# A hybrid-attention layer on one core: TensorE in program order along a reckoned clock, attention in three tasks

## The chip, the cores and the metric

The kernel runs on one core of one Trainium2 chip. The metric is device time in microseconds (us), the median of three runs; less is better. Beside each run stands one profiled execution with its trace.

## The reference

One layer of a streaming encoder for 1088 tokens: 1024 of a new prompt and 64 of a stream that goes on, with 512 cached tokens. Everything is fp32.

```python
h = x + 0.5 * rmsnorm(swiglu(rmsnorm(x, g_pre_ff1), w_gate1, w_up1, w_down1), g_post_ff1)
m, rows = token_mix(rmsnorm(h, g_pre_mix), ...)
h = h + rmsnorm(m, g_post_mix)
h = h + 0.5 * rmsnorm(swiglu(rmsnorm(h, g_pre_ff2), w_gate2, w_up2, w_down2), g_post_ff2)
return rmsnorm(h, g_final), rows
# swiglu: (silu(x @ w_gate) * (x @ w_up)) @ w_down        1024 -> 2816 -> 1024
# token_mix: 8 heads of latent attention (softmax, masked by chunks of 64 tokens) and 8 heads of
#   stick-breaking attention (strictly causal, weights from a reversed running sum of log sigmoids),
#   an RMS norm for each head, and one output projection
```

## The kernel before

**Numbers.** Every fp32 operand of a large product is split into a high and a low part (`split`, L121 and L122), and a product is three matmuls (`mm3`): high by high, high by low, low by high. `mul` (L132, L133) issues one matmul, `turn_over` (L137) one transpose on TensorE.

**Groups and stages.** The tokens are two groups: G1 with 576 tokens (moving chunks of 288) and G2 with 512 (one chunk). Two streams of work share TensorE: the feed-forward blocks, whose sums lie in the four PSUM buffers of tile `f`, and the mixing block (norms, projections, attention, output projection) in the single buffers of the tiles `v`, `t` and `s`. Below, F is a matmul of the feed-forward stream, and M is one of the mixing stream. By time: first feed-forward of G1 (0 to 447 us); mixing of G1 beside the first feed-forward of G2 (447 to 1161); mixing of G2 beside the second feed-forward of G1 (1161 to 1967); second feed-forward of G2 (1967 to the end).

**What sets the order.** `weave` takes steps of the mixing stream and puts steps of the feed-forward stream between them, by shares of counted work (`SHARE`). This is the order in which the program is written; the Tile scheduler then orders the instructions of every engine, TensorE's too, when the program is built, and each engine runs its list in that order. The feed-forward block stops before its last second-product part until the mixing block beside it is through (`while end and not self.mixed: yield None`).

**Feed-forward (`ffn`).** For two tiles of 128 hidden features at a time: gate and up products, silu, and the second product (`down`), which sums two tiles in PSUM (six matmuls) and is then added to y by VectorE (L265). Weights come as 128x512 loads `wr` (L241) that ScalarE and VectorE split into `wh` and `wl`.

**Mixing of a group.** `project` makes queries, keys and values, and stores keys and values to DRAM (the last ones by `latent_kv`, L451 and L452). `attend` walks over pairs of heads: `load_keys` reads the keys back from DRAM and splits them (L465 to L473), scores go to tile `s` on TensorE, `stick` (L510 to L532) or `soft` make weights `a` out of them on ScalarE and VectorE (three buffers `a`), and `weighted` turns the weights over (tile `t`), splits them into `ph` (ScalarE, L563) and `pl` (VectorE, L564), and multiplies with the values (tile `v`). `headnorm` sums squares in tile `v`. `mix_out` makes the output projection, a norm over its features, and then, for each of eight tiles of features, `residual`: a load of the saved h into `e` (L232), y * r (L233), y + e (L234), a store of the new h (L796), and a sum of squares (L186, L187). The SP queue has the next load `e<-h` behind the store of the tile before:

```python
nc.sync.dma_start(x, res)                                                    # L232
nc.vector.scalar_tensor_tensor(y, y, self.gain(name, k), r, ...)             # L233
eng.tensor_tensor(y, y, x, op=ALU.add)                                       # L234
if gi == 0: nc.sync.dma_start(self.h2[:, k], y[:, k])                        # L796, in mix_out
self.square(tmp, r2, y[:, k], k == 0)
```

`rsqrt` puts the sum of squares through TensorE with a matrix of ones (`v<-acc,ones` after the output projection, `s<-rx,ones` after the residual, `<-tmp,ones` at the start of a mixing block).

Of the kernel before, what the change touches and what calls it, by code (L numbers as in the profile page):

```python
# [7 lines left out]
F32 = mybir.dt.float32  # L8
# [7 lines left out]
P = 128  # L16
# [18 lines left out]
# token groups: (first token, tokens, chunk of the moving axis). The tokens lie as  # L35
# the first half of the prompt, the sample, the second half of the prompt.
# [4 lines left out]
# TensorE work of the feed-forward stream for one unit of the mixing stream's, part by part  # L41
SHARE = (0.1, 1.5, 0.1, 0.1, 1.2, 0.1)
PACE = 1.0
# [6 lines left out]
class Layer:  # L50
    def __init__(self, tc, ctx, a):
# [5 lines left out]
        self.work = self.share = self.debt = 0.0  # L57
        self.pace = PACE
# [26 lines left out]
        # keys and values: group 1 (prompt | new), group 2, cached  # L85
# [28 lines left out]
    # x = hi + lo exactly; without x, lo holds the value and is replaced in place  # L114
# [12 lines left out]
    # TensorE work is counted, for the interleaving of the two streams  # L127
    def mul(self, out, lhsT, rhs, start, stop):
# [3 lines left out]
        self.work += n / 2400 * (4 if rhs.dtype == F32 else 1)  # L132
        self.nc.tensor.matmul(out, lhsT=lhsT, rhs=rhs, start=start, stop=stop)  # L133

    def turn_over(self, out, x, ident):
        self.work += 0.1
        self.nc.tensor.transpose(out, x, ident)  # L137
# [5 lines left out]
    # a step without TensorE work in the first stream makes room for some of the second's  # L143
    def breath(self):
        self.debt += self.pace
        return True

    # the steps of the first stream, with the second one's between them: self.share of its work each
    def weave(self, first, second):
        mark = self.work  # L150
        for _ in first:
            self.debt += (self.work - mark) * self.share
            mark = self.work
            while self.debt > 0 and next(second, None):
                self.debt -= self.work - mark
                mark = self.work
# [7 lines left out]
    # a bank of the feed-forward stream  # L164
# [3 lines left out]
    # a bank of the mixing stream  # L168
# [10 lines left out]
    # sum of squares, tile by tile  # L179
# [9 lines left out]
    # 1 / sqrt(mean over all features + eps), on every partition, from the sums of squares  # L189
# [9 lines left out]
    # the same with the sums over the tiles left to TensorE (T at most 512)  # L199
# [10 lines left out]
    # tmp() gives [P, T] tiles  # L210
    def rms(self, tmp, bank, tiles, T, width, r=None):
# [33 lines left out]
    def ffn(self, pool, tmp, n, g, xhi, xlo, y, end=None, tail=None):  # L245
# [51 lines left out]
        while end and not self.mixed:  # L297
            yield None
# [799 lines left out]
```

## Time and profile before

| | |
|---|---|
| time, median of 3 (range) | 2368.68 us (2367.98 to 2368.76) |
| span of the profiled execution | 2367.6 us |
| TensorE: matmuls / weight loads | 2283.5 us (96%) / 2033.4 us (86%), 13869 of each |
| VectorE | 1539.0 us (65%) |
| ScalarE | 1244.7 us (53%) |
| GpSimd | 93.6 us (4%) |
| HBM | 227.61 MB read, 40.88 MB written, 113 GB/s over the span |

The profiled execution's span and the median of the runs lie 1.1 us apart. Busy times are sums over the span; matmuls overlap their weight loads, and a matmul that waits inside the engine's pipeline still counts as busy. The chain of work that ended last is TensorE for 69%, VectorE for 12%, ScalarE for 9%, and DMA for 4% of the span.

### The profile page before, as it was taken

The numbers are of one execution on the slowest core, as the hardware profiler recorded it, in microseconds if no ns is written. First come the engines' busy times: TensorE is split into PE (matmuls) and PEld (weight loads), VectorE is DVE, ScalarE is ACT, GpSimd is POOL, SyncE is SP. The second block draws the span as 40 slices with busy tenths as digits, with TensorE's granted clock in tenths as the row PEclk, the third lists the DMA queues.
The fourth block names the chain that finished last, engine by engine and source line by source line (L and its number), as shares of the span: only waits on it lengthen the run. The fifth ranks groups of instructions, "written<-read, shape, count | busy, mean of one in ns | idle before, by whom it ended". The sixth has DMA issues, their size and how long they took to land.

```text
span 2367.6 us, 37687 instructions
## 1 busy us (share of the span) xinstructions
PE 2283.5 (96%) x13869; PEld 2033.4 (86%) x13869; DVE 1539.0 (65%) x2743; ACT 1244.7 (53%) x2459; POOL 93.6 (4%) x270
## 2 busy tenths in 40 slices
PE   8999999989999999999999999999999999999997
PEld 7999999879987777788778999998888888888885
DVE  5555555764277878855873488888878588555555
ACT  6543333453367777754542477777776455433333
POOL 1000000010000000000110000000000010000001
PEclk9999999999999999999999999999999999999998
DMA  6322222445453343343444632323221424333321
GB/s 210 97 95 90 81 80 90 148 144 168 161 150 113 110 129 100 95 151 111 151 142 160 188 96 79 99 72 99 72 86 62 144 81 139 128 98 98 98 90 36
DMA packets 186615, 268.81 MB, mean 114 GB/s; under 512 B 59216, under 2 KB 68048, under 8 KB 186400
## 3 DMA queue, kind: packets, MB, share of 16 engines
q1 hardware_dynamic: 186432, 266.41, 35.8%
q8 instruction: 110, 1.80, 0.3%
q14 instruction: 73, 0.60, 0.1%
HBM read 227.61 MB, written 40.88 MB: 113 GB/s over the span
## 4 chain that ended last, share of the span: by engine, by line
PE 69%; DVE 12%; ACT 9%; DMA 4%; issue 4%; SPq 1%; POOL 1%; DVEq 0%; ACTq 0%; POOLq 0%
PE f L133 46%; PE s L133 11%; PE v L133 6%; PE t L133 3%; PE t L137 2%; DVE a L526 2%; DVE a L529 1%; ACT wh L121 1%; DVE a L520 1%; ACT a L517 1%; DVE wl L122 1%; ACT a L518 1%; ACT a L519 1%; DVE y L265 1%; DVE e L224 1%
## 5 line engine op out<-in xcount | busy, mean ns | idle before, releaser
L133 PE MATMUL f<-xh,wh 128*128 128x288 f32 (+1 forms) x2112 | 695.3, 329 | 4.4 <-ACT xh L121 2.8
L133 PE MATMUL f<-xl,wh 128*128 128x288 f32 (+1 forms) x2112 | 694.3, 329 | 2.9 <-POOL xl L122 1.8
L133 PE MATMUL f<-xh,wl 128*128 128x288 f32 (+1 forms) x2112 | 692.8, 328 | 0.0
L121 ACT CAST wh<-wr 128x512 fp32r<-128x512 f32 x638 | 374.2, 617 | 524.9 <-PE f L133 376.5
L122 DVE TENSOR_TENSOR wl<-wr,wh 128x512 fp32r<-128x512 f32 x638 | 431.2, 698 | 233.0 <-ACT wh L121 208.7
L133 PEld LDWEIGHTS f<-xl,wh 128*128 128x128 f32 x2112 | 397.7, 188 | 33.7 <-POOL xl L122 3.4
L133 PEld LDWEIGHTS f<-xh,wh 128*128 128x128 f32 x2112 | 397.6, 188 | 33.3 <-ACT xh L121 3.3
L133 PEld LDWEIGHTS f<-xh,wl 128*128 128x128 f32 x2112 | 397.5, 188 | 28.1 <-issue 0.8
L133 PE MATMUL f<-hh,wh 128*128 128x288 f32 (+2 forms) x1072 | 350.7, 328 | 6.6 <-ACT hh L121 3.2
L133 PE MATMUL f<-hl,wh 128*128 128x288 f32 (+2 forms) x1072 | 350.7, 327 | 0.0
L133 PE MATMUL f<-hh,wl 128*128 128x288 f32 (+2 forms) x1072 | 349.9, 327 | 0.2 <-DVE wl L122 0.2
L265 DVE TENSOR_TENSOR y<-f,y 128x288 f32<-128x288 f32 (+2 forms) x488 | 247.9, 523 | 85.4 <-PE f L133 83.8
L133 PEld LDWEIGHTS f<-hh,wh 128*128 128x128 f32 x1072 | 201.7, 189 | 23.4 <-ACT hh L121 4.0
L133 PEld LDWEIGHTS f<-hh,wl 128*128 128x128 f32 x1072 | 202.1, 189 | 14.3 <-issue 1.0
L133 PEld LDWEIGHTS f<-hl,wh 128*128 128x128 f32 x1072 | 202.1, 189 | 13.8 <-issue 0.8
L293 DVE TENSOR_TENSOR act<-f,act 128x288 f32<-128x288 f32 (+1 forms) x132 | 70.0, 531 | 92.6 <-PE f L133 91.8
L564 DVE TENSOR_TENSOR pl<-t,ph 128x384 fp32r<-128x384 f32 (+1 forms) x160 | 101.2, 633 | 35.6 <-ACT ph L563 31.2
L563 ACT CAST ph<-t 128x384 fp32r<-128x384 f32 (+1 forms) x160 | 86.7, 542 | 57.2 <-PE t L137 54.7
L292 DVE TENSOR_TENSOR act<-f,act 128x288 f32<-128x288 f32 (+1 forms) x132 | 69.8, 529 | 66.5 <-ACT act L291 66.4
L137 PE MATMUL t<-c_ident,a 128*128 128x128 f32 x616 | 106.0, 277 | 2.7 <-ACT a L531 0.9
L133 PE MATMUL s<-kh,qh 128*128 128x256 f32 (+3 forms) x224 | 84.4, 378 | 24.0 <-DVE a L529 16.1
L121 ACT CAST hh<-act 128x288 fp32r<-128x288 f32 (+1 forms) x132 | 64.8, 491 | 66.0 <-DVE act L293 65.9
(312 smaller groups left out, 3464.7 us busy)
## 6 DMA issues: line engine op xcount, KB each, us to landing
wr<-in_wg SPq DMA_DIRECT2D x176, 256.0 KB, 2.9
wr<-in_wu SPq DMA_DIRECT2D x176, 256.0 KB, 3.0
wr<-in_wd SPq DMA_DIRECT2D x176, 256.0 KB, 3.2
wr<-in_win SPq DMA_DIRECT2D x44, 256.0 KB, 3.3
kl<-ks SPq DMA_DIRECT2D x64, 128.0 KB, 2.8
wr<-in_wout SPq DMA_DIRECT2D x32, 256.0 KB, 2.8
h<-y SPq DMA_DIRECT2D x16, 288.0 KB, 2.3
p<-in_xT SPq DMA_DIRECT2D x16, 256.0 KB, 3.4
```

What stands on the lines that cost most here:

```text
L121: nc.scalar.copy(hi, x)
L122: eng.tensor_tensor(lo, x, f(hi), op=ALU.subtract)
L133: self.nc.tensor.matmul(out, lhsT=lhsT, rhs=rhs, start=start, stop=stop)
L137: self.nc.tensor.transpose(out, x, ident)
L224: self.nc.vector.scalar_tensor_tensor(x, src(k), self.gain(name, k), r, op0=ALU.mult, op1=ALU.mult)
L265: nc.vector.tensor_tensor(yy, ps[:, :C], yy, op=ALU.add)
L292: nc.vector.tensor_tensor(s, pg[:, :C], s, op=ALU.mult)
L293: nc.vector.tensor_tensor(s, pu[:, :C], s, op=ALU.mult)
L517: nc.scalar.activation(av, z, AF.Abs)
L526: nc.vector.tensor_tensor_scan(a[:, j0:n - 1][:, ::-1], zz[:, ::-1], a[:, j0:n - 1][:, ::-1], BIG, op0=ALU.add, op1=ALU.subtract)
L563: nc.scalar.copy(ph[:, end:], tr[:, end:])
L564: nc.vector.tensor_tensor(pl[:, end:], tr[:, end:], f(ph[:, end:]), op=ALU.subtract)
```

## The change

TensorE's order is no longer the scheduler's: the program runs under a manual schedule for that engine, which then executes its instructions as written; the other engines are scheduled as before. `weave`, the shares and the debts go. In their place a clock is kept that adds a price for each matmul. `wait(t)` issues feed-forward steps until the clock reaches t; if the feed-forward stream has no step to give, the clock is set to t. `done(t)` is the same with 4 us of head start (`AHEAD`). Norms, residuals and projections wait at reckoned times. `attend` becomes three tasks, each with a due time: `blocks` (scores and weights, up to six buffers `a`, `RING`), `products` (transposes and the product with the values), and `normed` (the norms of the heads, whose sum of squares now lies in tile `t`). The due task of the lowest number goes next; if none is due, `wait` pulls feed-forward steps. In the feed-forward blocks the second product sums four tiles of hidden features in PSUM (`GROUP`, twelve matmuls) where it summed two, weights are kept in units of 512 columns with eight buffers, and hidden tiles with five.

```diff
-SHARE = (0.1, 1.5, 0.1, 0.1, 1.2, 0.1)
+GROUP = 4
+AHEAD = 4.0
+RING = 6
+SLACK = 1.15
+EARLY = 8
+BLOCKED = object()
...
-    def weave(self, first, second):
-        for _ in first:
-            self.debt += (self.work - mark) * self.share
-            mark = self.work
-            while self.debt > 0 and next(second, None):
-                self.debt -= self.work - mark
-                mark = self.work
+    def wait(self, t):
+        while self.clock < t:
+            mark = self.clock
+            if next(self.filler, BLOCKED) is BLOCKED:
+                self.clock = max(t, mark)
+
+
+    def done(self, t):
+        self.wait(t - AHEAD)
+        return t
...
-        for m in range(0, FT, 2):
+        def product(part, ws, first, dt, c0, C):
+            ps = self.bank_f()
+            ks = slice(dt % H * P, dt % H * P + P)
+            for i, ((wh, wl), (_, hh, hl)) in enumerate(zip(ws, part)):
+                self.mm3(ps[:, :C], wh[:, ks], wl[:, ks], hh[:, c0:c0 + C], hl[:, c0:c0 + C],
+                         i == 0, i == len(part) - 1)
+            yield True
...
+        def down(part, first):
+            for half in range(2):
+                ws = [self.unit(pool, wd[mi][:, half * 512:half * 512 + 512]) for mi, _, _ in part]
+                for dt in range(half * H, half * H + H):
+                    for c0 in range(0, T, C):
+                        yield from product(part, ws, first, dt, c0, C)
...
+        for m in range(0, FT, GROUP):
+            for mi in range(m, min(m + GROUP, FT)):
+                if mi == m + 1 and pend:
+                    yield from down(pend.pop(0), m == GROUP)
...
         while end and not self.mixed:
-            yield None
+            yield BLOCKED
-        yield from down(pend.pop(0), False, order, end)
+        yield from down_last(pend.pop(0), tail, end)
...
+        nc = self.nc
+        a = pool.tile([P, self.keys], F32, name="a", bufs=RING)
...
+    def chain(self, mla, n):
+        act, dve = n / 1200 + 0.35, n / 960 + 0.25
+        if mla:
+            t = 0.6 + dve + act + 0.3
+            return SLACK * t, SLACK * t
+        t = 0.8 + 3 * act + dve + 2 * dve + 0.2
+        return SLACK * t, SLACK * (t + act)
...
         for j in range(0, tiles, 2):
             t = turned(j)
-            yield
+            self.used += 2 if j + 2 == tiles else 0
             if pend:
                 product(*pend)
-                yield
+            yield self.clock + SLACK * 1.9
...
+            e = self.sum_rows(pool, total.rearrange("p b h -> p (b h)"), 4)
+            turned = self.psa.tile([P, 4, P], F32, name="t")
+            for b in range(4):
+                self.turn_over(turned[:, b], e[:, b].rearrange("p h d -> p (h d)"), self.ident)
+            turned = turned.rearrange("p b q -> p (b q)")
...
-        ps = self.psa.tile([P, 512], F32, name="v")
+        yield self.clock + SLACK * (0.3 + n / 500)
+        ps = self.psa.tile([P, 512], F32, name="t")
...
+        first, second, third = ([self.clock, g] for g in (self.blocks(pool, gi), self.products(), self.normed()))
+        while True:
+            tasks = []
+            if first[1] and self.made - self.used < RING:
+                tasks.append((first[0], 0, first))
+            if second[1] and (self.going or self.queue):
+                tasks.append((second[0] if self.going else max(second[0], self.queue[0][0]), 1, second))
+            if third[0] is not None and (self.norming or self.norms):
+                tasks.append((third[0] if self.norming else max(third[0], self.norms[0][0]), 2, third))
+            if not tasks:
+                break
+            due = [t for t in tasks if t[0] <= self.clock]
+            if due:
+                task = min(due, key=lambda t: t[1])[2]
+                task[0] = next(task[1], None)
+                if task[0] is None:
+                    task[0], task[1] = 0.0, None
+            else:
+                self.wait(min(t[0] for t in tasks))
...
+                free, there = self.chain(mla, n)
+                there += self.clock
+                    self.queue.append((there, self.weighted(pool, ab, v, par, b0 + 2 * qp + 2, out, par, then)))
+                self.made += 1
+                yield self.clock + free
...
+        self.wait(self.clock + SLACK * (3 * T / 1000 + 1.0))
         self.rsqrt(bank, s1, T, D, s1)
...
-            yield self.breath()
+            t = self.done(t + SLACK * (2.7 * T / 960 + 0.4))
+        self.wait(t + 2.0)
         self.rsqrt(bank, r2, T, D, r2)
...
-    sizes = {"wr": 4, "wl": 4, "wh": 4, "hh": 3, "hl": 3}
+    sizes = {"wr": 4, "wl": 8, "wh": 8, "hh": GROUP + 1, "hl": GROUP + 1}
...
-    L.weave(mix0(), first)
+
+    first = L.ffn(F, fact, 1, G2, *x1, y1, end=prep2)
+    L.filler = first
+    at = finish(0, y0, 1, L.bank_m)
...
-        with ExitStack() as ctx:
+        with ExitStack() as ctx, tc.manual_schedule(engines={mybir.EngineType.PE}):
```
What the change does to TensorE's list where the first scores of G2's attention are. `wh, lh, ll` are the weights and latent of the last projection (values), `kh, qh` the keys and queries of the first head, `xh, xl` the feed-forward's input. Before:

```order
L133 MATMUL s<-wh,lh 128x512
L133 MATMUL s<-wh,ll 128x512
L133 MATMUL s<-wl,lh 128x512
L133 MATMUL f<-xl,wh 128x288
L133 MATMUL f<-xh,wl 128x288
L133 MATMUL f<-xh,wh 128x288
```

These three F rows are the first of 121 that stand there before the first `s<-kh,qh`. With the change:

```order
L148 MATMUL s<-wh,lh 128x512
L148 MATMUL s<-wh,ll 128x512
L148 MATMUL s<-wl,lh 128x512
L148 MATMUL s<-kh,qh 128x320
L148 MATMUL s<-kh,ql 128x320
L148 MATMUL s<-kl,qh 128x320
```

The 121 F rows between the last projection and the first scores are gone from this place. In G1's attention it is the same with 46 F rows.

TensorE's list after G1's output projection, between the norm over its features (`acc,ones`) and the norm over the new h (`rx,ones`). Before, the first rows of it, and the last:

```order
L133 MATMUL v<-acc,ones 128x288
L133 MATMUL t<-acc,ones 128x288
L133 MATMUL f<-hl,wh 128x512
L133 MATMUL f<-hh,wl 128x512
...
L133 MATMUL f<-hl,wh 128x512
L133 MATMUL s<-rx,ones 128x288
```

With the change, all of it:

```order
L148 MATMUL v<-acc,ones 128x288
L148 MATMUL t<-acc,ones 128x288
L148 MATMUL f<-xh,wh 128x512
L148 MATMUL f<-xl,wh 128x512
L148 MATMUL f<-xh,wl 128x512
L148 MATMUL f<-xh,wh 128x512
L148 MATMUL f<-xl,wh 128x512
L148 MATMUL f<-xh,wl 128x512
L148 MATMUL f<-xh,wh 128x512
L148 MATMUL f<-xl,wh 128x512
L148 MATMUL f<-xh,wl 128x512
L148 MATMUL s<-rx,ones 128x288 x2
```

There were 151 F rows between the two norms, and now there are nine. From there to the next norm (`v<-tmp,ones`) there are now 108, and between the same two norms of G2 (`acc,ones` to `rx,ones`) 159.

SP's queue at the same place, with the loads of the saved h (`h_0`) and the stores of the new one. Before:

```order
L232 DMA e<-h_0_71 128x576 x2
L796 DMA h_73<-y 128x576 x2
L232 DMA e<-h_0_71 128x576
L796 DMA h_73<-y 128x576
L232 DMA e<-h_0_71 128x576
L241 DMA wr<-in_wd 128x512 x2
L796 DMA h_73<-y 128x576
```

With the change:

```order
L254 DMA e<-h_0_73 128x576 x2
L272 DMA wr<-in_wu 128x512
L930 DMA h_75<-y 128x576 x2
L254 DMA e<-h_0_73 128x576
L930 DMA h_75<-y 128x576
L254 DMA e<-h_0_73 128x576
L272 DMA wr<-in_wu 128x512
L930 DMA h_75<-y 128x576
```

A load of h still stands behind the store of the tile before; the weight loads between them are fewer.

TensorE's list in G1's attention, where a head's norm comes due (`osq` squares, `c_blk` the matrix that sums them, `c_ident` the transposes). With the change:

```order
L148 MATMUL v<-aT,v 128x64 x10
L152 MATMUL t<-c_ident,a 128x128 x3
L148 MATMUL t<-osq,c_blk 128x512
L148 MATMUL s<-kh,qh 128x512
L148 MATMUL s<-kh,ql 128x512
```

The norm's sum, which stood in tile `v`, stands in the one buffer of tile `t` right behind transposes into it. 17 of the 24 norms of both attentions stand so.

## Rows read from the trace of the kernel before

**Rows 1.** The page: span, busy time of each engine, and the additions into y.

```profile
span 2367.6 us, 37687 instructions
PE 2283.5 (96%) x13869; PEld 2033.4 (86%) x13869; DVE 1539.0 (65%) x2743; ACT 1244.7 (53%) x2459; POOL 93.6 (4%) x270
...
L265 DVE TENSOR_TENSOR y<-f,y 128x288 f32<-128x288 f32 (+2 forms) x488 | 247.9, 523 | 85.4 <-PE f L133 83.8
```

**Rows 2.** Windows by stage, whole core; the columns are in the first line.

```profile
core 0: us, PE busy (x) PEld busy (x) DVE busy (x) ACT busy (x) POOL busy (x), PEclk, DMA share, GB/s
447.00:650.20 203.20, 194.01 (x1222) 174.30 (x1221) 98.01 (x152) 84.13 (x161) 9.30 (x6) 0.99 0.49 161
650.20:661.00 10.80, 10.63 (x48) 8.47 (x46) 4.79 (x9) 5.41 (x11) 0.70 (x6) 1.00 0.61 173
661.00:1035.00 374.00, 365.53 (x1879) 289.17 (x1880) 297.29 (x603) 269.98 (x614) 17.46 (x118) 1.00 0.40 117
...
1096.10:1136.20 40.10, 36.10 (x156) 28.53 (x154) 31.55 (x49) 18.93 (x33) 4.49 (x2) 1.00 0.58 182
1136.20:1174.20 38.00, 36.35 (x190) 30.67 (x190) 32.73 (x48) 23.72 (x46) 5.98 (x4) 1.00 0.32 101
...
1335.10:1351.10 16.00, 16.00 (x123) 16.00 (x122) 10.07 (x19) 9.39 (x21) 0.00 (x0) 1.00 0.85 239
1351.10:1837.50 486.40, 467.67 (x3329) 437.93 (x3328) 397.51 (x708) 348.05 (x623) 14.39 (x96) 1.00 0.28 85
...
1902.30:1931.90 29.60, 27.50 (x200) 26.53 (x199) 27.73 (x49) 14.97 (x30) 3.41 (x2) 1.00 0.37 116
```

**Rows 3.** Windows of two stretches with feed-forward alone, 288 and 512 wide.

```profile
200.00:400.00 200.00, 200.00 (x1511) 200.00 (x1510) 104.12 (x207) 72.27 (x151) 0.00 (x0) 1.00 0.26 85
2100.00:2200.00 100.00, 100.00 (x443) 82.81 (x442) 50.83 (x79) 33.95 (x61) 0.00 (x0) 1.00 0.30 98
```

**Rows 4.** Timeline from G2's last projection to its first scores (start us, us, engine, line).

```profile
1334.83 0.39 PE L133 MATMUL s<-wl,lh 128*128 128x512 f32 x1
...
1335.31 0.69 DVE L451 COPY e<-s 128x512 f32<-128x512 f32 x1 [0.32 <-PE s L133]
...
1348.69 1.05 ACT L121 CAST kh<-kl 128x1024 fp32r<-128x1024 f32 x1
```

**Rows 5.** Timeline of SP's queue in the residual after G1's output projection.

```profile
1108.07 0.32 SPq L796 DMA_DIRECT2D h<-y  x1
1108.48 0.38 SPq L232 DMA_DIRECT2D e<-h  x1
...
1112.29 0.33 SPq L796 DMA_DIRECT2D h<-y  x1
...
1134.63 0.32 SPq L796 DMA_DIRECT2D h<-y  x1
```

**Rows 6.** Windows of tile f alone: residual of G1, the next norm, the residual of G2.

```profile
1096.10:1136.20 40.10, 35.51 (x151) 28.11 (x151) 8.55 (x14) 1.18 (x2) 1.00 0.58 182
1136.20:1174.20 38.00, 35.72 (x185) 30.09 (x185) 8.64 (x14) 1.41 (x3) 1.00 0.32 101
...
1902.30:1931.90 29.60, 27.00 (x197) 26.18 (x196) 6.80 (x17) 1.22 (x3) 1.00 0.37 116
```

**Rows 7.** Waits of PE in the two attentions: us in total, times, longest.

```profile
PE s L133 <- DVE a L526: 6.5, 18, 0.6
...
PE s L133 <- DVE a L529: 15.8, 25, 2.0
```

**Rows 8.** One line's instructions: duration ns min/median/max, L563 and L564.

```profile
L563 ACT CAST ph<-t x160: 459/579/601, 667.4 to 1832.9; 128x512 fp32r<-128x512 f32 x96, 128x384 fp32r<-128x384 f32 x64
...
L564 DVE TENSOR_TENSOR pl<-t,ph x160: 529/680/693, 667.9 to 1833.4; 128x512 fp32r<-128x512 f32 x96, 128x384 fp32r<-128x384 f32 x64
```

**Rows 9.** Windows around the start of G2's mixing; PEclk is the granted clock.

```profile
1190.00:1197.00 7.00, 4.35 (x33) 4.04 (x31) 5.95 (x9) 2.87 (x6) 1.44 (x1) 1.00 0.79 258
1197.00:1203.80 6.80, 4.95 (x15) 3.95 (x16) 5.77 (x12) 5.13 (x11) 0.00 (x0) 0.52 0.67 221
```

More of the change, by code (lines that the diff above doesn't have):

```diff
@@ L56, in __init__ @@
         self.turn = 0
-        self.work = self.share = self.debt = 0.0
-        self.pace = PACE
+        self.clock = 0.0
+        self.filler = iter(())
         self.mixed = False
@@ L608, in headnorm @@
         nc.sync.dma_start(self.o_s[gi][row * P:row * P + P, c0:c0 + n], sq[:, :n])
+        yield self.clock
     def attend(self, pool, gi):
         self.keys, self.ahead = ((576, 4), (1024, 2))[gi]
[L612 to L618 removed]
+        self.queue, self.norms, self.made, self.used = [], [], 0, 0
@@ new lines, in products, with normed, blocks @@
+    def products(self):
+        while True:
+            self.going = False
+            yield self.clock
+            self.going = True
+            yield from self.queue.pop(0)[1]
+    def normed(self):
+        while True:
+            self.norming = False
+            yield self.clock
+            self.norming = True
+            yield from self.norms.pop(0)[1]
+    def blocks(self, pool, gi):
+        kinds = [(pair, kind) for pair in range(4) for kind in ("mla", "sb")]
+        heads = []
+        for pair, kind in kinds:
+            heads += [(pair, kind, "prompt", 0), (pair, kind, "prompt", 1)] + ([(pair, kind, "sample", None)] if gi == 0 else [])
+        ready = None
+        made = [self.load_head(pool, gi, *heads[0])]
+        for i, (pair, kind, what, par) in enumerate(heads):
+            ops, v = made.pop(0)
+            if par == 0:
+                o = pool.tile([P, 512], F32, name="o")
+                total = pool.tile([P, 4, 2], F32, name="total") if kind == "mla" else None
+                vv = v
+            if i + 1 < len(heads):
+                made.append(self.load_head(pool, gi, *heads[i + 1]))
+            if what == "sample":
+                yield from self.sample_pair(pool, kind, pair, ops, v)
+            else:
+                yield from self.prompt_head(pool, kind, pair, par, gi, 4 * gi, ops, vv, o, total)
@@ L737, in sample_pair, with sample_products @@
             nc.gpsimd.memset(t[:, n - 1:n], 0.0)
+        free, there = self.chain(mla, n)
+        self.queue.append((self.clock + there, self.sample_products(pool, mla, pair, t, v, total)))
+        self.made += 1
+        yield self.clock + free
+    def sample_products(self, pool, mla, pair, t, v, total):
+        nc = self.nc
         aT = pool.tile([P, 5, P], F32, name="aT")
@@ new lines, in body @@
+    with tc.tile_pool(name="a0", bufs=2) as ap:
+        L.attend(ap, 0)
+    mp = opened.enter_context(tc.tile_pool(name="o0", bufs=1))
+    tmp, wp, acc = work(mp, T1, 3)
+    o = pair(mp, T1, "o")
+    h2.append(mp.tile([P, KT, T1], F32, name="y"))
+    L.mix_out(wp, tmp, acc, L.bank_m, 0, G1, *o, h2[0], rx)
+    L.mixed = True
+    L.run(first)
+    y2 = ytile(T1)
+    second = L.ffn(F, fact, 2, G1, *x2, y2)
+    L.filler = second
+    rz = fp.tile([P, TM], F32, name="rx")[:, :T2]
+    at = finish(1, y1, 1, L.bank_m)
```

483 lines of the change are left out of this document (229 added, 254 removed).

## The prediction

> **What bounds the kernel now.** I read the page's busy times first. TensorE is busy for 2283.5 of 2367.6 us, VectorE for 1539.0 and ScalarE for 1244.7 [rows 1]. So TensorE bounds the kernel, and what it sits idle is 84.1 us in all: an order that filled every hole could gain no more than that, unless time is lost inside its busy time too.
>
> Next I cut the span at the stages and read the windows [rows 2], to see where the 84 us are. The two attentions hold 374.00 − 365.53 = 8.5 and 486.40 − 467.67 = 18.7 us of idle time, the residual after G1's output projection 40.10 − 36.10 = 4.0, the two stretches in which the first head's keys go through DRAM 0.2 and 0.0, and the front of G1's mixing 203.20 − 194.01 = 9.2. The waits of the attentions have one main cause each: scores that wait until the tile `s` has been read by VectorE's running sum, 6.5 and 15.8 us [rows 7].
>
> Last I asked what covers the long chains off TensorE. Between G2's last projection at 1334.83 and the first scores at the end of that window, at 1351.1, lie a copy, a store to DRAM, loads and splits; the keys' cast begins only at 1348.69 [rows 4]. TensorE is busy for all 16.00 us of it, and 121 F matmuls do that. In the residual of G1 TensorE is busy for 36.10 of 40.10 us, and 35.51 of it are 151 F matmuls [rows 6]. These are holes that F fills today, and so the places to look at in the new order.
>
> **The change, part by part.** The sum is made against the profiled execution: span 2367.6 us, and 1.1 us more to the median of the runs, 2368.7.
>
> First scores. The new order has no F between the last projection and the first scores, in either attention. TensorE takes its list in order, so it stands still while the keys are on their way. Nothing of the path itself changes, so today's windows bound it from above: 10.8 + 16.0 = 26.8 us. Part of the path stands behind splits of feed-forward weights on ScalarE and VectorE, which are busy for 9.39 and 10.07 of the 16.0 us; where TensorE stands still these thin out. If a third of the path were such delay it would be 18. I take 23, nearer to the row than to the guess. **+23 (18 to 27).**
>
> Residual of G1. Now nine F matmuls stand there. Today's take 35.51 / 151 = 0.235 us each, so nine give 2.1 us, and the two norms' sums 36.10 − 35.51 = 0.6. The path is a ring through SP's queue: from one store of h (1108.07) the next load goes out at 1108.48, and the next store can go at 1112.29, 4.2 us later; the last goes at 1134.63 [rows 5]. The new order leaves each load behind the store before it, so the ring stays. Of the 40.10 us I take off VectorE's 8.55 us on tile `f` [rows 6], which now come elsewhere: 31.6. That leaves 31.6 − 2.7 = 28.9 idle where 4.0 are today. **+25.** If the ring takes today's time it is 40.1 − 2.7 − 4.0 = +33; if VectorE's own work alone is left, 31.55 − 8.55 = 23.0, it is +16.
>
> The two stretches behind. From that norm to the next, 108 F matmuls at today's 35.72 / 185 = 0.193 us [rows 6] give 20.9 us, where VectorE has 32.73 − 8.64 = 24.1 us of work that isn't the feed-forward's sums: 24.1 − 20.9 − 0.6 leaves 2.6 idle, against 1.65 today. If the stretch kept its 38.0 us it would be 15 more. In the residual of G2, 159 F at 27.00 / 197 = 0.137 us give 21.8; with VectorE's 6.80 us taken off, the window shrinks to 22.8 and nothing is lost, with nothing taken off it is 29.6 − 21.8 − 0.5 − 2.1 = 5 more. **+5 (0 to 20).**
>
> Attention. Six buffers `a` and due times that let scores be issued only when `s` should be free can take away the waits for `s`: 6.5 + 15.8 = −22. Against that stands tile `t`: in 17 places a norm's sum goes into its one buffer right behind transposes, and has to wait until `pl` is read out, 0.68 us [rows 8]: 17 x 0.68 = +12. In the other direction there is time that doesn't show as idle. Feed-forward alone keeps the weight loads busy for 1.000 of the time at 288 wide and 0.828 at 512 wide [rows 3]; the attentions have 289.17 / 374.00 = 0.773 (G1, beside F 512 wide) and 437.93 / 486.40 = 0.900 (G2, beside 288 wide). Run like the feed-forward alone they would take 349.2 and 437.9 us, 24.8 + 48.5 = 73 less, of which 27 are the recorded idle time. The other 46 are an upper bound, since the attention's own matmuls have other widths; I take a quarter of it, −12, which offsets the +12. **−22 (−73 to +12).**
>
> The Trainium skill speaks for more. Its page "Trainium Kernel Development and Optimization", section Performance Expectations, says that the busy time of matmuls is a bad measure of how close a kernel is to its limit, because matmuls are pipelined, and that the busy share of the weight loads is a good one. By busy time the kernel has 4% left, by weight loads 14%. By that reading the attention's term would be the −73, and the sum 51 us lower.
>
> Front of G1's mixing: 9.2 us idle, which a feed-forward step at each reckoned time may halve. **−5 (−9 to +5).**
>
> Clock. TensorE was idle for 2.65 us of 1190 to 1197 and for 1.85 us of the window behind it, in which the granted clock was 0.52 (the 1.2 GHz level) for 4.95 us of matmuls [rows 9]. At full clock these would take 2.4 us less. Three new long holds (two first scores, one residual): 3 x 2.4 = **+7 (0 to 14,** none or twice as many, since the residual's hold may fall into pieces).
>
> Four tiles in PSUM: additions into y fall from 488 to 248, at 523 ns some 120 us of VectorE less [rows 1]. With feed-forward alone TensorE is busy for 200.00 of 200 us while VectorE has 104 [rows 3], so there they are hidden already, and I cost it at **0**; in the attentions it is part of what lets `s` come free sooner, and is counted there. The matmuls are as many as before, and the rest of the stages keeps its time.
>
> Sum: 23 + 25 + 5 − 22 − 5 + 7 = +33, and 2368.7 + 33 is **2402 us**. All ends low are 18 + 16 + 0 − 73 − 9 + 0 = −48 (2321), all high 27 + 33 + 20 + 12 + 5 + 14 = +111 (2480).
>
> **The rivals.**
>
> Faster. The attentions lose time inside busy TensorE, and an order by reckoned times takes all of it away: −73 in place of −22 gives 2351. It decides from the point where the attentions give back more than 22 + 33 = 55 us. For it speaks the weight loads' share of 0.90 in G2's attention, where feed-forward alone has 1.00 [rows 2, 3]; against it that transposes and scores of mixed widths don't reach the feed-forward's share. It is the rule of the skill's page above carried to its end; the trace bears out that there is a gap, not that the order can close it.
>
> The holes are smaller, since engines without feed-forward work run their chains faster: first scores 18, residual 16, the stretches behind 0, clock 2, so 18 + 16 + 0 − 22 − 5 + 2 = +9, 2378. For it speaks VectorE's 31.55 of 40.10 us busy in the residual [rows 2]; against it the ring through DRAM, in which one load is on its way at a time [rows 5].
>
> Slower still. The reckoned times are too short in the attentions too, and a matmul that comes up before its operand is there now holds all of F behind it: the 27 us of idle time double where I let 22 go. 2402 + 22 + 27 = 2451. For it speaks the residual: the program reckons 1.15 x (2.7 x 576 / 960 + 0.4) = 2.3 us for a step that takes 4.2 [rows 5]. Against it, the attention's products are reckoned from operations on chip, with 15% on top.
>
> That TensorE's order isn't changed can be left out: the rows of the order show it.
>
> **How the numbers follow.** The forecast with its own range of 2385 to 2425 gets 0.40, small holes 0.24, slower still 0.15, faster 0.16, and 0.05 goes to a case between small holes and faster that ends at today's time. A measurement of this kernel tells 0.2% (4.7 us) from no change. Small holes lie 0.4% above today, so a quarter of that case (0.06) counts as no change: 0.11 for the same, 0.16 for faster, and 0.73 for slower. The range runs from the faster case, half of which it leaves out, to just below the case slower still: 2352 to 2446.
>
> **What would show it.** In the changed kernel TensorE should be idle for about 10 and 13 us before the first scores of the attentions, and for some 29 us, in pieces, in G1's residual between the two norms, while SP alternates loads and stores of h at 4 us a pair. The granted clock should fall behind each of these. In the attentions the waits of `s` for the running sums should be nearly gone, with short waits of `t` for `pl` in their place. Additions into y should be 248. The prediction is wrong if the weight loads' share in G2's attention comes near 1.0 (then the attention gives back more than the holes cost), or if the residual takes less than 25 us.

## The result and the profile after

The changed kernel takes 2509.16 us (median, 2507.76 to 2509.99) against 2368.72 us: a ratio of 1.0592, with a 95% interval of 1.0577 to 1.0607. The sign was forecast, the size was not: +140 us where +33 was worked out, and outside the range of 2352 to 2446.

The page of the changed kernel, its lines that answer to [rows 1]:

```profile
span 2508.2 us, 37563 instructions
PE 2302.5 (92%) x13869; PEld 2078.3 (83%) x13869; DVE 1439.6 (57%) x2498; ACT 1277.4 (51%) x2464; POOL 92.2 (4%) x270
...
L297 DVE TENSOR_TENSOR y<-f,y 128x288 f32<-128x288 f32 (+2 forms) x248 | 127.9, 518 | 136.2 <-PE f L148 135.3
```

The span is 140.6 us longer. TensorE runs the same 13869 matmuls; it is busy 19.0 us longer and idle for 205.7 us where it was 84.1. VectorE has 99 us less to do, and nothing comes of it. So most of the time, 121.6 us, went into TensorE's idle time, and the windows by stage, cut at the same places of the program as [rows 2] (behind the last projection, before the first scores, and so on), say where:

```profile
core 0: us, PE busy (x) PEld busy (x) DVE busy (x) ACT busy (x) POOL busy (x), PEclk, DMA share, GB/s
446.50:670.60 224.10, 202.90 (x1243) 182.56 (x1242) 100.27 (x154) 84.52 (x161) 10.38 (x6) 0.97 0.45 149
670.60:680.70 10.10, 0.03 (x1) 0.03 (x1) 1.59 (x4) 2.63 (x5) 0.70 (x6) 0.59 0.60 158
681.00:1117.00 436.00, 415.45 (x2094) 346.55 (x2094) 297.69 (x599) 288.85 (x643) 17.35 (x118) 0.97 0.36 106
1117.00:1188.40 71.40, 62.80 (x423) 59.76 (x422) 27.23 (x44) 27.04 (x49) 0.00 (x0) 0.95 0.35 114
1188.40:1223.30 34.90, 3.22 (x15) 2.27 (x13) 18.99 (x25) 8.38 (x14) 2.79 (x2) 0.59 0.42 134
1223.30:1253.80 30.50, 25.19 (x112) 20.72 (x112) 24.85 (x35) 17.33 (x31) 5.69 (x4) 0.85 0.17 58
...
1289.80:1424.20 134.40, 121.39 (x609) 101.35 (x607) 50.38 (x78) 40.62 (x76) 3.06 (x3) 0.96 0.44 145
1424.20:1436.30 12.10, 0.02 (x1) 0.02 (x1) 2.57 (x5) 3.88 (x7) 0.00 (x0) 0.60 0.63 176
1436.50:1975.00 538.50, 513.57 (x3688) 494.32 (x3689) 393.58 (x673) 378.82 (x678) 14.24 (x96) 0.98 0.28 82
1975.00:2037.00 62.00, 53.05 (x248) 44.13 (x247) 26.57 (x45) 20.41 (x36) 0.00 (x0) 0.94 0.38 123
2037.00:2068.90 31.90, 22.21 (x164) 21.50 (x162) 25.17 (x42) 11.78 (x21) 4.00 (x2) 0.89 0.37 116
```

Three stretches of the kernel before, which the prediction took to keep their time, in the same view (output projection of G1, projections of G2, output projection of G2):

```profile
1035.00:1096.10 61.10, 60.93 (x424) 58.04 (x423) 27.96 (x45) 23.27 (x43) 0.00 (x0) 1.00 0.34 111
1198.80:1335.10 136.30, 134.65 (x719) 114.92 (x720) 61.09 (x93) 51.92 (x103) 5.67 (x4) 0.98 0.47 152
1837.50:1902.30 64.80, 62.95 (x334) 54.63 (x332) 32.68 (x56) 25.20 (x46) 0.00 (x0) 1.00 0.38 126
```

Duration less PE busy, after and before, gives the idle time that each stage gained, beside the term of the sum:

| stage | idle before | idle after | gained | forecast |
|---|---|---|---|---|
| first scores, G1 and G2 | 0.2 + 0.0 | 10.1 + 12.1 | +22.0 | +23 |
| residual of G1 | 4.0 | 31.7 | +27.7 | +25 |
| next norm, and residual of G2 | 1.7 + 2.1 | 5.3 + 9.7 | +11.2 | +5 |
| attentions | 8.5 + 18.7 | 20.6 + 24.9 | +18.3 | −22 |
| front of G1's mixing | 9.2 | 21.2 | +12.0 | −5 |
| projections of G2, output projections | 1.7 + 0.2 + 1.9 | 13.0 + 8.6 + 9.0 | +26.8 | 0 |
| TensorE busy (in the sum: the clock) | 2283.5 | 2302.5 | +19.0 | +7 |

These make 137.0 of the 140.6 us. The waits that stand behind them, over the whole span of the changed kernel (us in total, times, longest):

```profile
PE s L148 <- DVE rx L199: 31.7, 1, 31.7
PE t L148 <- DVE pl L619: 19.9, 17, 2.2
PE v L148 <- ACT wh L133: 16.5, 4, 7.4
PE t L152 <- DVE pl L619: 13.1, 11, 1.9
PE s L148 <- DMA kl<-kr: 12.1, 1, 12.1
...
PE s L148 <- ACT qh L136: 10.1, 1, 10.1
PE t L148 <- DVE rx L199: 9.7, 1, 9.7
...
PE s L148 <- ACT a L588: 3.0, 6, 0.9
```

The waits of `s` for running sums, 22.3 us in [rows 7], are gone from the list; the 3.0 us of L588 are waits for the softmax to read `s`. Tile `t` waits for `pl` in their stead, 33.0 us. G1's residual is one wait of 31.7 us; in it SP's queue still sends one load behind each store (L254 loads, L930 stores):

```profile
1199.18 0.32 SPq L930 DMA_DIRECT2D h<-y  x1
1199.59 0.38 SPq L254 DMA_DIRECT2D e<-h  x1
...
1203.47 0.32 SPq L930 DMA_DIRECT2D h<-y  x1
1203.88 0.38 SPq L254 DMA_DIRECT2D e<-h  x1
1208.26 0.32 SPq L930 DMA_DIRECT2D h<-y  x1
```

That is 4.3 and 4.8 us a pair, where it was 4.2 in [rows 5].

The 19.0 us of busy time are the balance of two larger changes. The windows over all stretches in which the granted clock was 0.50 (the 1.2 GHz level) have these sums; there are six such stretches before, and 28 with the change:

```profile
sum 33.75, PE 24.39 PEld 19.16 DVE 21.55 ACT 16.46 POOL 6.03; mean PE 4.07 PEld 3.19 DVE 3.59 ACT 2.74 POOL 1.01
sum 197.40, PE 120.22 PEld 97.87 DVE 104.77 ACT 74.90 POOL 13.32; mean PE 4.29 PEld 3.50 DVE 3.74 ACT 2.68 POOL 0.48
```

F matmuls 288 wide start 0.24 us apart at this level, as behind the first scores of G2, and 200 / 1511 = 0.132 us apart at the upper level (granted clock 1.00, the 2.4 GHz level, [rows 3]):

```profile
1439.05 0.44 PE L148 MATMUL f<-xl,wh 128*128 128x288 f32 x1
1439.29 0.44 PE L148 MATMUL f<-xh,wl 128*128 128x288 f32 x1
```

So some 0.45 of the busy time at the lower level is the price of that level. The busy time there grew from 24.4 to 120.2 us, and 0.45 x 95.8 makes 43 us, an estimate. The rest of the busy time must then have fallen by some 24 us. The longest stretches lie in the three long waits (34.1 us in G1's residual, 13.7 us at each of the first scores). Ten of 3.4 to 6.8 us lie in the attentions. Nine of them begin within a wait of `t` for `pl` of 1.2 to 2.2 us, or at most 1.4 us behind it, and the tenth at a wait of `t` for `osq` of 1.1 us; other waits as long had no such stretch behind them. One of them, its wait by the timeline and the stretch by windows:

```profile
801.50 0.43 PE L148 MATMUL t<-osq,c_blk 128*128 128x64 f32 x2 [1.83 <-DVE pl L619]
802.09:805.50 3.41, 3.41 (x10) 2.64 (x9) 0.55 (x2) 0.45 (x2) 0.00 (x0) 0.50 0.33 89
```

### The profile page after: what moved, and what is told of

The parts are those of the page before. It is cut to its first block, busy times and chain, and to the rows that moved or that the text cites. A ratio compares the mean times of both kernels' runs of the same rounds, so it can differ in the third digit from the quotient of the medians.

```text
span 2508.2 us, 37563 instructions
## 1 busy us (share of the span) xinstructions
PE 2302.5 (92%) x13869; PEld 2078.3 (83%) x13869; DVE 1439.6 (57%) x2498; ACT 1277.4 (51%) x2464; POOL 92.2 (4%) x270
## 4 chain that ended last, share of the span: by engine, by line
PE 59%; DVE 7%; ACT 7%; DMA 3%; issue 3%; SPq 1%; POOL 1%; DVEq 0%; ACTq 0%; POOLq 0%
PE f L148 35%; PE s L148 10%; PE v L148 6%; PE t L148 4%; PE t L152 2%; ACT wh L133 1%; DVE a L572 1%; DVE e L242 1%; DVE pl L619 1%; DVE wl L134 1%; DMA e<-h 1%; ACT a L564 1%; ACT a L565 1%; ACT a L563 1%; DVE y L255 0%
## 5 line engine op out<-in xcount | busy, mean ns | idle before, releaser
L148 PE MATMUL f<-xh,wh 128*128 128x288 f32 (+1 forms) x2112 | 707.2, 335 | 3.6 <-ACT xh L133 3.6
L133 ACT CAST wh<-wr 128x512 fp32r<-128x512 f32 x638 | 383.4, 618 | 528.0 <-PE f L148 341.2
L134 DVE TENSOR_TENSOR wl<-wr,wh 128x512 fp32r<-128x512 f32 x638 | 436.5, 698 | 246.5 <-ACT wh L133 207.2
L148 PE MATMUL f<-hh,wh 128*128 128x288 f32 (+2 forms) x1072 | 357.5, 333 | 4.5 <-ACT hh L133 4.5
L148 PEld LDWEIGHTS f<-hl,wh 128*128 128x128 f32 x1072 | 205.1, 191 | 16.3 <-DVE hl L134 1.9
L297 DVE TENSOR_TENSOR y<-f,y 128x288 f32<-128x288 f32 (+2 forms) x248 | 127.9, 518 | 136.2 <-PE f L148 135.3
L152 PE MATMUL t<-c_ident,a 128*128 128x128 f32 x616 | 98.1, 276 | 10.6 <-DVE pl L619 5.7
L148 PE MATMUL s<-kh,qh 128*128 128x256 f32 (+3 forms) x224 | 80.6, 362 | 25.7 <-DMA kl<-kr 12.1
```

The source lines that it names most:

```text
L133: nc.scalar.copy(hi, x)
L134: eng.tensor_tensor(lo, x, f(hi), op=ALU.subtract)
L297: nc.vector.tensor_tensor(yy, ps[:, :C], yy, op=ALU.add)
```

## The experiments

Theory: the whole loss comes from TensorE's program order, which lays open chains that the scheduler covered with feed-forward matmuls, one hole at a time. Rival: the three tasks, the six buffers, or the four-tile sum lose it. Runs without an interval are one execution each, beside the kernel before on the same chip (2362 to 2372 us); differences of a few us between them carry nothing.

### Order, or the rest of the change

**e1_scheduler**

```diff
-        with ExitStack() as ctx, tc.manual_schedule(engines={mybir.EngineType.PE}):
+        with ExitStack() as ctx:
```

> The changed kernel, with TensorE's order given back to the scheduler and all else of the change kept. Theory (TensorE's program order is the loss: it exposes chains that other feed-forward matmuls used to cover): TensorE idle falls from 206 to below 110 us and the time to 2350 to 2390. Rival (the loss comes from the three tasks, the six buffers or the four-tile sum): the time stays above 2470.

2369.43 us, ratio 1.0013 (1.0003 to 1.0023). One line gives back all 140 us; idle time falls to 97.1. The rest of the change, as it stands, is worth nothing in sum. That is the balance of a gain and a loss: less their F matmuls the two attentions take 39 us less than before (the working is in the next section), while G1's residual is idle for 22.6 of 36.7 us where 4.0 were. Its waits are of another kind:

```profile
PE s L148 <- DVE rx L199: 18.2, 1, 18.2
PE f L148 <- DVE y L297: 15.4, 3, 9.6
...
PE t L152 <- DVE pl L619: 2.8, 7, 0.6
```

The scheduler hides `t`, the weights and the first scores; the hole in G1's residual stays, since little feed-forward work is left there.

**e2_four_tiles**: the kernel before with the new `ffn` and its buffers.

```diff
-        for m in range(0, FT, 2):
+        for m in range(0, FT, GROUP):       # GROUP = 4
```

> The kernel before, with the feed-forward block of the change alone (four tiles summed in PSUM, weights in units of 512 columns, five hidden tiles). Theory (the additions into y were hidden): 2355 to 2375, VectorE some 120 us less busy. Rival (a bank is held for twelve matmuls and the order around it gets coarser, so the attentions lose): above 2395.

2369.14 us, ratio 1.0011 (1.0001 to 1.0021); VectorE is busy for 1435.4 us, 104 less. Cost and gain of the sum in PSUM are nil there, as forecast. (e2 has the change's smaller DMA scratch, `dynamic_dma_scratch_size=1024`, too; so has e16. No run tests that alone.)

**e3_old_weave_in_order**: the kernel before, with the manual schedule of TensorE as its only edit.

> The kernel before, its program unchanged, with TensorE held to program order. Theory (program order in itself is what costs, since the old weave puts a product right behind the weights that it waits for): 2550 to 2900, TensorE idle for over 250 us. Rival (the reckoned clock and its due times are what costs): below 2480.

3122.44 us; beyond the theory's figure even. TensorE is idle for 630 us, most of it in the attentions, in waits for their weights `a` (36 transposes wait 174.1 us for one line alone):

```profile
PE t L137 <- ACT a L531: 174.1, 36, 7.5
PE s L133 <- DVE a L529: 93.1, 16, 6.5
PE s L133 <- DVE a L526: 53.5, 16, 3.9
```

So program order costs 755 us with the old weave, and the reckoned clock takes back 613 of them (3122 to 2509). The clock isn't what loses; it doesn't reckon enough.

### The holes one by one, in program order

**e4_filler_before_scores**

```diff
         self.going = self.norming = False
+        self.wait(self.clock + (13.0, 15.0)[gi])
```

> The changed kernel with 13 and 15 us of feed-forward steps asked for between the last projection and the first scores of the attentions. Theory (the hole of 11.5 + 13.5 us is idle time that feed-forward can fill): 2475 to 2490, the two long waits gone. Rival (the feed-forward matmuls that are spent here are missing at the end of the same mixing block, where the hole grows by as much): 2500 to 2512.

2484.59 us, 24.6 less. Both waits, 22.2 us, are gone from the list; in G1's residual the wait grows only from 31.7 to 34.0. That the gain is about the size of the waits is chance in part: idle time falls by 11.0 us only (other waits grow, as that of `v` for `wh` from 16.5 to 19.0), and busy time by 14.4. The busy time at the lower clock level falls from 120.2 to 86.9 us, by the rate above worth some 15. So the rival is right in half of the idle time, and the holes cost time behind them too, through the clock.

**e5_norm_in_f**

```diff
-        ps = self.psa.tile([P, 512], F32, name="t")
+        ps = self.bank_f()
```

> The changed kernel, with the sum of squares of a head's norm in a bank of tile f in place of the single buffer of t. Theory (waits of t for the reading of the transposes are what replaced the waits of s): the norms' waits of 19.9 us for pl go, 2485 to 2495. Rival (they only cover waits of the transposes behind them, which then wait for the same reading): 2502 to 2512, the waits of the transposes for pl grow by as much.

2478.90 us, 30.3 less, more than the 19.9 us of waits. The transposes' waits for `pl` stay (13.9 for 13.1), so the rival is out; TensorE's busy time falls by 11.7 us, which is the part beyond the waits; some 6 of it are the clock (106.0 us busy at the lower level for 120.2).

**e6_residual_ahead**

```diff
-            self.residual(tmp(), y[:, k], "postmix", k, s1, self.h1[gi][:, k], nc.gpsimd if k % 3 == 2 else nc.vector)
+            while len(saved) < min(KT, k + 3):
+                x = self.saved(T)
+                nc.sync.dma_start(x, self.h1[gi][:, len(saved)])
+                saved.append(x)
+            self.residual(saved[k], y[:, k], "postmix", k, s1, None, nc.gpsimd if k % 3 == 2 else nc.vector)
```

> The changed kernel, with the loads of the saved h in three buffers of their own and issued two tiles ahead, so that no load stands behind the store of the tile before. Theory (the hole of 31.7 us in the residual of G1 is the ring load, add, store through SP's queue): the hole shrinks to 14 to 20 us and the time to 2490 to 2500. Rival (VectorE's own work sets the hole): it shrinks by less than 5 us, 2503 to 2512.

2488.99 us, 20.2 less. The wait for `rx` falls from 31.7 to 18.3: the ring through SP's queue was 13 us of the hole, and in the other 18 the additions and squares follow one another on VectorE, GpSimd and ScalarE. In G2's residual the wait of 9.7 us for `rx` goes too, and 3.5 us of idle time are left there. (The edit also takes one buffer of work tiles from G1's output projection; e16 has this too.)

**e10_in_order_three_mended**: e4, e5 and e6 together.

> The changed kernel in program order with the three edits of the single runs together: feed-forward before the first scores, norms in banks of f, loads of h two tiles ahead. Theory (three separate holes, each idle time of its own): the gains add, 24.6 + 30.3 + 20.2, 2428 to 2442. Rival (they share the same feed-forward work, so that what one fills opens another): 2450 to 2480.

2437.90 us: 71.3 less, where the single runs sum to 75.1. These three are holes of their own.

**e11_slack_one**

```diff
-SLACK = 1.15
+SLACK = 1.0
```

> The changed kernel with the factor on reckoned times at 1.0 in place of 1.15. Theory (the attention's reckoned times are too short already where tile t is reused): waits of t for pl rise from 33 to over 45 us, the hole in G1's residual shrinks by under 10, and the time is 2500 to 2525. Rival (the factor spends feed-forward work in the attention that the residual then lacks): the hole shrinks by over 15 us, 2475 to 2495.

2512.68 us. Neither was right in its parts. Waits of `t` for `pl` are 29.0, not over 45, with 5.6 more of `v` for `pl`; the hole in G1's residual shrinks by 18.5 to 13.2, as the rival had it, but the time doesn't follow. What the shorter reckoning leaves for the residual, it takes from other waits: this step of the factor moves idle time, and gains none.

**e12_two_t_three_f**: `psf` with three banks, tile `t` with two.

```diff
-        self.psf = ctx.enter_context(tc.tile_pool(name="psf", bufs=4, space=PSUM))
+        self.psf = ctx.enter_context(tc.tile_pool(name="psf", bufs=3, space=PSUM))
-            tr = self.psa.tile([P, 4, P], F32, name="t")
+            tr = self.psa.tile([P, 4, P], F32, name="t", bufs=2)
```

> The changed kernel with two buffers of tile t and three of tile f. Theory (the one buffer of t is the cause of the waits of 19.9 + 13.1 us for pl): they fall below 8 us, 2468 to 2485. Rival (with three banks the feed-forward itself waits for its banks to be read): 2495 to 2530.

2456.30 us, 52.9 less, the largest single edit. Waits of `t` for `pl` fall from 33.0 to 3.5. Idle time falls by 28.7 and busy time by 25.0, so the list of waits showed little more than half of the loss. The other part goes with the clock: the busy time at the lower level falls from 120.2 to 73.4 us, by the rate above worth 21 of the 25.

```profile
sum 143.04, PE 73.37 PEld 61.70 DVE 67.38 ACT 50.44 POOL 9.47; mean PE 4.32 PEld 3.63 DVE 3.96 ACT 2.97 POOL 0.56
```

Of the ten short stretches at that level in the attentions none is left. The three banks of `f` cost nothing that shows.

**e13_in_order_four_mended**: e4, e6 and e12 together, and in `mix_out`

```diff
-                    self.wait(there - (6.0 if k < KT - 1 else 0.0))
+                    self.wait(there)
```

> Program order with feed-forward before the first scores, loads of h two tiles ahead, two buffers of t and three of f, and 13 in place of 7 us of feed-forward before the first matmul of the output projections. Theory (separate holes): 24.6 + 20.2 + 52.9 and 11 of the 14 us of waits for the first weights, so 2400; 2392 to 2410. Rival (the feed-forward work runs out, and the residual of G2, with 66 F matmuls for 159, loses what is gained): 2412 to 2430.

2433.77 us, 34 above the sum. The idle times of e4, e6 and e12 do add: 11.0 + 14.3 + 28.7 = 54.0 us, and e13 has 54.1 less than the changed kernel. Their busy times don't: 14.4 + 6.7 + 25.0 = 46.1 us, and e13 has 22.1 less. The three runs counted the clock's gain more than once: their busy time at the lower level is 33.3, 17.3 and 46.8 us less, and that of e13 only 39.2 less (81.0 us). These are 24 of the 34 us. Most of the other 10 are the last edit, of which 11 were asked: the waits of `v` for `wh` are 13.6 us, and 16.3 in e12. The residual of G2 waits 9.7 us for `rx`, as it did in the changed kernel, so the rival's mechanism isn't shown, though its figure was right.

**e14_in_order_spared**: e13, and the attentions may not take the last 24 and 20 feed-forward steps (`L.spare`).

```diff
-            if next(self.filler, BLOCKED) is BLOCKED:
+            if self.left <= self.spare or next(self.filler, BLOCKED) is BLOCKED:
```

> The run before it, with the last 24 (G1) and 20 (G2) feed-forward steps kept from the attentions. Theory (the wait that is left in G1's residual is missing feed-forward work): it falls below 8 us, 10 to 20 us under the run before it. Rival (the attention in program order needs these steps): within 5 us of it or above.

2427.52 us. The wait in G1's residual falls from 18.6 to 8.0, 10.6 us, and the time by 6.3; the steps that are kept back are mostly, not wholly, paid for in the attention, where a new wait of 5.1 us for a running sum appears. In program order the best is thus 2.6% over the kernel before.

### The scheduler's order, with the holes mended

**e7_scheduler_residual_ahead** is e1 with the edit of e6, **e8_scheduler_spared** is e1 with 48 and 30 steps kept back as in e14, **e9_scheduler_both** has the loads ahead and 24 and 20 steps kept back.

> The scheduler's order of TensorE with the loads of the saved h two tiles ahead. Theory (in the run with the scheduler's order the wait of 18.2 us in G1's residual is the last large loss, and it is the ring): 2350 to 2360. Rival (the time lies in feed-forward work that is merely moved): 2364 to 2374.

> The scheduler's order of TensorE, and the attentions may not take the last 48 (G1) and 30 (G2) steps of the feed-forward stream beside them; these are left for the residual. Theory (the hole is the absence of feed-forward work): the wait in G1's residual falls from 18.2 to under 6 us, 2345 to 2360. Rival (the attention needs these steps to cover its own chains): 2364 to 2380.

> The scheduler's order of TensorE, the loads of the saved h two tiles ahead, and the last 24 (G1) and 20 (G2) feed-forward steps kept for the residuals. Theory (both mend the same hole, of which 11.6 and 4.0 us are left): 2343 to 2354. Rival (the attention needs the steps that are kept back): 2355 to 2365.

| run | us (range) | ratio to before (95%) |
|---|---|---|
| e7 | 2355.59 (2349.73 to 2360.12) | 0.9960 (0.9946 to 0.9974) |
| e8 | 2358.09 (2353.16 to 2361.16) | 0.9966 (0.9952 to 0.9981) |
| e9 | 2346.19 (2343.73 to 2347.90) | 0.9916 (0.9902 to 0.9929) |

e8 left a wait of 11.8 us for `rx`, so its first part missed. e9 beats both kernels: 0.8% below the kernel before, 6.5% below the change. The windows of its two attentions:

```profile
670.90:1050.00 379.10, 378.17 (x1984) 315.06 (x1984) 286.01 (x584) 277.88 (x628) 17.52 (x118) 1.00 0.39 118
...
1335.20:1830.00 494.80, 486.18 (x3541) 467.26 (x3540) 383.52 (x657) 366.85 (x662) 14.12 (x96) 1.00 0.28 88
```

They hold 9.6 us of idle time, where the kernel before has 27.2, and the weight loads' share is 0.831 and 0.944, where it was 0.773 and 0.900.

**e15_scheduler_two_t**: e9 with the buffers of e12.

> The scheduler's order with loads of h ahead and steps kept back, and two buffers of t, three of f. Theory (the scheduler puts other work where t is not free, so the second buffer is worth only the 5 us of waits seen there): 2336 to 2348. Rival (three banks hold the feed-forward back where the scheduler used four): 2352 to 2375.

2348.57 us, ratio 0.9924 (0.9910 to 0.9938): e9's time. The second buffer is worth 53 us to a fixed order and nothing to the scheduler.

**e16_before_residual_ahead**: the kernel before with the edit of e6. **e17_scheduler_both_two_tiles**: e9 with `GROUP = 2`.

> The kernel before, with the loads of the saved h two tiles ahead and nothing else. Theory (in the kernel before 151 feed-forward matmuls cover the ring, and TensorE is idle for 4.0 us there): 2362 to 2370. Rival (the ring is what the best version mends, under any order): 2345 to 2358.

> The best version (the scheduler's order, loads of h ahead, steps kept back) with two tiles of hidden features summed in PSUM, as before the change. Theory (the additions into y are hidden): 2341 to 2354. Rival (in the attentions VectorE's extra 120 us delay the scores): 2358 to 2375.

e16: 2379.00 us, ratio 1.0062 (1.0041 to 1.0083). The loads ahead alone don't help the kernel before, they cost 0.6%; neither account had that. In its trace G2's residual is idle for 7.7 us where 2.1 were, and the busy time at the lower clock level is 41.1 us for 24.4; why wasn't found. e17: 2365.43 us, ratio 0.9995 (0.9985 to 1.0004), so without the four-tile sum the 0.8% are gone. The rival's figure was right: the sum in PSUM that is worth nothing in the kernel before is worth 19 us in this order. Its mechanism isn't shown: scores wait 5.3 us for the running sums, and 5.6 in e9. Less their F matmuls the attentions take 8.5 us more than in e9, and the busy time at the lower clock level is 55.1 us for 42.6. A step of the second product is half as long with two tiles, so the steps that are kept back hold less work in e17; how much of the 19 us that is wasn't separated.

## Why the prediction was wrong

**Right in kind and size.** First scores (+23 forecast, +22.0 idle); the residual of G1 (+25 forecast, +27.7; e6 shows the ring in it, but only for 13 us, and the program's 2.3 us a step against 4.3 measured). The two stretches behind, +11.2, lie within their bounds of 0 to 20, but 7.6 of it are in G2's residual, which was put at nothing and where e6 shows the ring again. The four-tile sum at 0 holds in e2, not in e17. All that was to show the forecast came (first scores, residual, pairs of loads and stores, waits of `t`, 248 additions), and neither of its two signs of being wrong did. None of them put a size on the three steps below, in which the forecast failed.

**The first step that failed: the attentions at −22 us.** The waits of `s` did go, 22.3 us. What took their place was priced as 17 x 0.68 = +12, and offset against hidden stalls. The price was too low twice over in idle time. A sum behind transposes waits for `ph` and then `pl`, 0.58 + 0.68 = 1.26 by [rows 8], and 17 of them took 19.9 us, 1.17 each. Transposes behind them wait too, 13.1 us in eleven places that the order's rows didn't show as a problem. The term was about +18 in idle time, outside its own bound of +12. The −12 for time hidden in busy TensorE was right in kind and too small: some 24 us of busy time went, by the estimate above, and the clock took them back.

**The second, a term put at nothing: "the rest of the stages keeps its time".** It did under the scheduler, and couldn't in program order. The projections of G2 and the two output projections gained 26.8 us of idle time, the front of G1's mixing 12.0 where −5 was put: first weights that aren't split yet (`v` for `wh`, 16.5 us in 4 waits) and banks that aren't read yet. I looked for holes where the order had lost its feed-forward rows, and not where a product now stood right behind its own operand. e3 shows what that costs unreckoned: 755 us.

**The third, the term most mis-sized: the clock at +7 (0 to 14).** It was priced as three long holds of 2.4 us each. The granted clock did fall there (0.59 in G1's residual, 0.85 in the stretch behind, 0.59 and 0.60 at the first scores), but it was at its lower level in 28 stretches where six were, and the busy time in them is 95.8 us more: some 43 us, as estimated above. The short waits in the attentions and before projections were enough for it, and the sum had no term for that. Some 24 us less of other busy time hide it in the table.

**The rivals.** "Slower still" (2451) had the right mechanism, a late operand that now holds all of the feed-forward behind it, and was still too small. The faster rival's gap is real: a time in attention less its F matmuls at 0.2257 us (512 wide) and 0.1324 us (288 wide) from [rows 3] is 143.1 + 206.6 = 349.7 us before, by [rows 2, 6] and 1023 and 2113 F matmuls; in e9, with 1128 and 2325 of them, it is 124.5 + 187.0 = 311.5, 38 us less of the 73 that were the bound. In e1, without the mended holes, it is 310.7 already (1146 F of 382.4 us, 2307 of 492.4), in e17 320.0. In the change's own order the same sum is 156.6 + 211.2 = 367.8 (1238 and 2472 F). But that isn't the order's fault alone: e12, in program order with the second buffer of `t`, has 125.0 + 191.8 = 316.8 (1244 and 2473 F). So the three tasks do win the time back, in either order, once `t` doesn't hold them; the rival had its mechanism right, and the buffer and the clock took the gain.

The F counts are those of the windows of tile `f` alone; of the changed kernel, of e9 and of e12:

```profile
681.00:1117.00 436.00, 312.20 (x1238) 232.78 (x1239) 43.10 (x63) 13.49 (x23) 0.97 0.36 106
1436.50:1975.00 538.50, 363.43 (x2472) 340.97 (x2473) 53.08 (x119) 20.47 (x51) 0.98 0.28 82
```

```profile
670.90:1050.00 379.10, 283.39 (x1128) 204.96 (x1128) 40.36 (x59) 11.09 (x19) 1.00 0.39 118
1335.20:1830.00 494.80, 338.02 (x2325) 315.97 (x2324) 50.01 (x112) 19.85 (x49) 1.00 0.28 88
```

```profile
682.20:1088.00 405.80, 306.00 (x1244) 228.47 (x1245) 43.75 (x64) 13.53 (x23) 0.99 0.38 115
1403.80:1923.00 519.20, 359.80 (x2473) 338.16 (x2474) 53.28 (x119) 20.58 (x51) 0.99 0.28 86
```

And of the kernel before:

```profile
661.00:1035.00 374.00, 263.15 (x1023) 183.70 (x1024) 57.39 (x85) 8.30 (x14) 1.00 0.40 117
...
1351.10:1837.50 486.40, 310.48 (x2113) 288.43 (x2112) 75.42 (x176) 11.82 (x29) 1.00 0.28 85
```

The rule of the Trainium skill that I weighed ("Trainium Kernel Development and Optimization", Performance Expectations: judge by the weight loads' busy share, not by that of the matmuls) came out well here. By busy time there was little left in the attentions; by weight loads there was more, and e9 got half of it, with the shares rising as told above. In the changed kernel the shares rose too, to 0.795 and 0.918, while the time went up: the share says what is left, not that an order will get it.

Open: e16's loss, why the lower clock level stays in e13, and how the 19 us of e17 divide. That the clock's price is 43 us rests on one rate for all matmuls at the lower level; it is an estimate.

## What to carry to other kernels

When an engine's order is taken from a scheduler, price every place in which an instruction stands right behind its own operand, and not only those from which the cover was taken: here the first kind cost some 57 us of idle time (attentions, front, projections), the second 61. Price the clock by all of the waits and not by the longest alone: here it came to some 43 us. A reckoned order needs slack in buffers more than in its factors: a second PSUM buffer gave 53 us, a change of the factor from 1.15 to 1.0 nothing. When the gains of single edits are to be added, add idle time and busy time apart; here the first added and the second didn't. And an edit that is worth nothing under one order can be worth 19 us under another (the four-tile sum), so try the parts of a change again once the order is settled.

## What the hardware showed that I had not expected

The busy time of the same 13869 matmuls runs from 2267.7 us (e9) over 2302.5 (changed) to 2491.2 us (e3, mean granted clock 0.886): an engine that is starved more is also busier. Most of it is the clock: at its lower level TensorE was busy for 42.6, 120.2 and 437.6 us in these three, and less 0.45 of that 2249, 2248 and 2294 us are left (2273 in the kernel before). An edit that took away 29.5 us of waits for `pl` (33.0 to 3.5) cut 52.9 us; in the attentions of the changed kernel the granted clock fell to 0.50 at waits of TensorE as short as 1.1 to 2.2 us, ten times.
